# Coefficients of an expert layer's second product, made in pairs of blocks and in place

## The chip, the cores and the metric

The kernel runs on one core of a Trainium2 chip. The metric is the time of one execution on the device, in microseconds; the median of the runs counts. A core has five engines that run side by side: TensorE (matrix products, PE in the profile), VectorE (DVE), ScalarE (ACT), GpSimd (POOL) and SyncE (SP). Each works through its own queue in order. Transfers between memory and the core run on 16 DMA engines; here SyncE's, ScalarE's and GpSimd's queues issue them.

## The reference

The model has two layers. Each has a mixer (a diagonal state-space part and a forgetting attention) and then an expert layer, "PEER", on 512 tokens of width 1024. The change lies in the expert layer:

```python
t1, i1 = lax.top_k(s1, 16); t2, i2 = lax.top_k(s2, 16)      # per token and head, 8 heads
...
best, pos = lax.top_k(cand, 16)                              # 16 of 16384 experts
gate = jax.nn.softmax(best, axis=-1)
...
act = gelu(einsum('tkd,td->tk', u_tab[idx], h))
out = einsum('tk,tkd->td', act * gate, v_tab[idx])
```

Each token takes 8 x 16 of 16,384 experts, each a row of `u_tab` and one of `v_tab`, and sums the rows of `v_tab` with the coefficients `gelu(u . h) * gate`.

## The kernel before, in words

The 512 tokens are four blocks of 128. For three of them (384 tokens, `NT`) the kernel computes the expert layer densely: all 16,384 experts, in 128 blocks of 128 (`NBLK`), with a gate that is zero for an expert that a token did not take. The fourth block of tokens gathers its rows one by one (`gather_step`, lines 974 to 986): an indirect load on GpSimd, a dot product on VectorE (line 995), a gelu and a scale on ScalarE (lines 996, 997) and a sum on VectorE (line 998). These steps are spread over the whole layer.

The dense part has two products. The first (`u_stage`, lines 928 to 938) makes, for one block of experts, the activations of 384 tokens: 128 partitions (experts) by 384 columns (tokens), gelu on ScalarE. For the first 116 blocks (`NAHEAD`, called `M`) this is done ahead, while the routing and the gates are computed, and the activations are written to memory (`ad`). The last 12 blocks, here called late, run inside the second part: their activations stay on the core.

The gates (`gates`) are written to memory as `gd`, laid out by 12 groups of 32 tokens, 128 experts of a block, 128 blocks, 32 tokens.

The second product (phase "two", lines 1051 to 1117) goes through an order of 140 steps, `order`: a late `u`, then 9 or 10 of the early `v` blocks, then the late `v`, twelve times over. For each `v` block:

- `gate_of` and `act_of` load gates and activations for four blocks at a time, on ScalarE's queue, each into one of two buffers (`g0`, `ar`); late gates go, also by four, into the one buffer `g1`. They are called for the block itself and up to four (`PF`) blocks on. `s.after(s.marks[0])` puts such an issue behind the last block's rounding on ScalarE.
- `v_coef` (lines 950 to 963) multiplies activation and gate on VectorE into `c` (one buffer, line 958), rounds it on ScalarE to the high half of `cc` (line 960), and subtracts on VectorE to get the low half (line 961). `cc` has three buffers of one block.
- `v_block` (lines 965 to 972) issues 6 matmuls for each of the three blocks of tokens, 18 in all, adding into six banks of PSUM, with the weights split the same way: `hi` on ScalarE (line 168), `lo` on VectorE or, for every fourth block, on GpSimd (line 169). `raw` has five buffers, loaded by SyncE (line 160); `hi` and `lo` have three each, and the next block's are made while one is in use.

In layer 0 the preparation of layer 1's state-space part (`s5_prep`) runs in small pieces in the same phase, mostly on VectorE, with small stores on ScalarE's queue. The order of the instructions on each engine is made by the framework: it takes the ready instruction of the highest priority in a run of its own clock. `high_priority(offset=AHEAD)` lets splits and coefficients go ahead of their place. A tile with `bufs=n` is handed out again once everything that used it is done.

```python
def v_coef(s, act, gate):
    c = s.t("c", [1, NT])
    cc = s.t("cc", [2, NT], F32R, bufs=3)
    ...
```

Of the kernel before, what the change touches and what calls it, by code (L numbers as in the profile page):

```python
# [9 lines left out]
F32R = mybir.dt.float32r  # L10
# [3 lines left out]
AF = mybir.ActivationFunctionType  # L14
OP = mybir.AluOpType
# [8 lines left out]
NT = 384  # L24
# [22 lines left out]
class Net:  # L47
# [899 lines left out]
                s.gather_step()  # L947
            yield

    def v_coef(s, act, gate):  # L950

        nc = s.nc
        v = nc.vector
        c = s.t("c", [1, NT])
        cc = s.t("cc", [2, NT], F32R, bufs=3)
        ch, cl = cc[:, 0], cc[:, 1]
        with s.tc.high_priority(offset=AHEAD):
            v.tensor_tensor(c[:, 0].rearrange("p (g t) -> p g t", t=32), act.rearrange("p (g t) -> p g t", t=32),  # L958
                            gate, op=OP.mult)
            on_act = nc.scalar.activation(ch, c[:, 0], AF.Copy)  # L960
            on_dve = v.tensor_tensor(cl, c[:, 0], ch, op=OP.subtract)  # L961
        s.marks = on_act, on_dve
        return ch, cl

    def v_block(s, w, c, tb, first, last):
        wh, wl = w
# [33 lines left out]
    def peer(s, prep_next):  # L1000
        nc, a, l = s.nc, s.a, s.l
# [10 lines left out]
        M = NAHEAD  # L1012
# [9 lines left out]
        ad = s.dr.tile([M, 128, NT], F32, name=f"ad{l}", tag="ad")  # L1022
# [28 lines left out]
        with s.phase("two"):  # L1051
            for _ in up:
                pass
            s.pv = [[s.p("pb"), s.p("pb")], [s.p("pb"), s.p("pb")], [s.p("pc"), s.p("pc")]]
            G, A = {}, {}

            def gate_of(b):
                key = (b // 4, b < M)
                if key not in G:
                    g = s.t("g0" if b < M else "g1", [NT // 32, 4, 32], bufs=2 if b < M else 1)  # L1060
                    q = b - b % 4
                    nc.scalar.dma_start(g, s.gd[:, :, q:q + 4].rearrange("g p i t -> p g i t"))
                    G[key] = g
                return G[key][:, :, b % 4]

            def act_of(b):
                if b >= M:
                    return A.pop(b)
                if b // 4 not in A:
                    t = s.t("ar", [4, NT], bufs=2)  # L1070
                    q = b - b % 4
                    nc.scalar.dma_start(t, ad[q:q + 4].rearrange("b p t -> p b t"))
                    A[b // 4] = t
                return A[b // 4][:, b % 4]

            nv = 0
            tail = []
            vs = [b for kd, b in order if kd == "v"]
            prep = iter(())
            if prep_next:  # L1080
                prep = s.s5_prep(l + 1, (nc.vector,), "pa", 1)
            for i, (kd, b) in enumerate(order):
                w = next(ws)
                if kd == "u":
                    o = s.ga.tile([128, NT], F32, name=f"au{l}_{b}", tag="ao", bufs=3)
                    s.u_stage(w, o)
                    A[b] = o
                else:
                    for fb in vs[nv:nv + PF + 1]:
                        with ExitStack() as st:  # L1090
                            if nv:
                                st.enter_context(s.after(s.marks[0]))
                            gate_of(fb)
                            if fb < M:
                                act_of(fb)
                    c = s.v_coef(act_of(b), gate_of(b))
                    nv += 1
                    if nv <= NBLK - TAIL:
                        for tb in range(NTB):
                            s.v_block(w, c, tb, nv == 1, False)  # L1100
                    else:
                        tail.append((w, c))
                gl = 128 + GLAG - GA
                if (i + 1) * gl // GEND > i * gl // GEND:
                    s.gather_step()
                if i >= 24 and i % PREPSTEP == 0:
                    with s.after(s.marks[0]), s.after(s.marks[1]):
                        next(prep, None)
            while s.gk < 128 + GLAG:
                s.gather_step()  # L1110
            list(prep)
            for tb in range(NTB):
                for j, (w, c) in enumerate(tail):
                    s.v_block(w, c, tb, False, j == TAIL - 1)
                for hf in range(2):
                    hs = s.h[:, tb, 512 * hf:512 * hf + 512]
                    nc.vector.tensor_tensor(hs, s.pv[tb][hf], hs, op=OP.add)
# [91 lines left out]
```

## Time and profile before

| | |
|---|---|
| median of 3 runs | 3212.95 us (3211.52 to 3228.48) |
| the profiled execution | 3227.44 us |
| its span, first to last instruction | 3225.7 us |
| mean granted TensorE clock | 0.986 |
| busy: TensorE, VectorE, ScalarE, GpSimd | 3111.4, 2379.7, 1156.8, 841.5 us |
| moved by DMA | 810.92 MB, 251 GB/s |

The span is one execution; the engines overlap, so the busy times do not add up to it. An engine's idle time counts only where another that sets the end waits for it. A matmul is pipelined: its busy time says when the array was occupied, not at what rate, so counts of matmuls in a stretch are the better measure of progress. "Granted clock" is the share of full speed at which TensorE was allowed to run. In rows about queues, ACTq is ScalarE's queue: the time an issue of a transfer holds it.

### The profile page before, as it was taken

What the parts mean: (1) busy time and instruction counts of PE and PEld (TensorE: products, weight loads), DVE (VectorE), ACT (ScalarE), POOL (GpSimd) and SP (SyncE); (2) the same over time, 40 slices, a digit from 0 to 9 for tenths busy, and PEclk for the clock granted to TensorE, in tenths of its full rate; (3) what the DMA queues carried; (4) which work ended last, traced back from release to release, by engine and by line L of the source; (5) the groups of instructions that cost most, each with busy time, mean ns of one, the idle gap of its engine ahead of it and who ended that gap; (6) DMA issues with size and microseconds to landing.
All of it is one profiled execution on the core that took longest, in us unless ns stands there. A gap on an engine that the chain in (4) does not pass through costs nothing. (4 is left out here: it accounts for less than half of the span.)

```text
span 3225.7 us, 43367 instructions
## 1 busy us (share of the span) xinstructions
PE 3111.4 (96%) x15858; PEld 2449.3 (76%) x15858; DVE 2379.7 (74%) x5007; ACT 1156.8 (36%) x2192; POOL 841.5 (26%) x488
## 2 busy tenths in 40 slices
PE   8999998999999998999999999989999999999998
PEld 7756755677999777787889576546779987788887
DVE  7654697977545798998767647979766367788887
ACT  3263212333333343444342531123333333334443
POOL 3100012101675332343210000210027742233231
PEclk9999998999999999999999999999999999999999
DMA  6511278767898889999963123887579889999995
GB/s 185 195 54 58 92 266 306 251 225 267 310 302 307 306 309 308 346 333 334 331 211 104 40 79 97 296 301 248 208 276 321 287 303 320 324 330 344 333 344 208
DMA packets 354726, 810.92 MB, mean 251 GB/s; under 512 B 22833, under 2 KB 228657, under 8 KB 318673
## 3 DMA queue, kind: packets, MB, share of 16 engines
q1 hardware_dynamic: 136608, 326.23, 30.5%
q0 software_dynamic: 36864, 268.45, 22.2%
q10 hardware_dynamic: 181040, 213.48, 19.7%
q8 instruction: 124, 2.03, 0.3%
q14 instruction: 90, 0.73, 0.1%
HBM read 693.19 MB, written 114.82 MB: 250 GB/s over the span
## 5 line engine op out<-in xcount | busy, mean ns | idle before, releaser
L169 POOL TENSOR_TENSOR lo<-raw,hi 128x1024 fp32r<-128x1024 f32 x160 | 429.5, 2688 | 1082.6 <-ACT hi L168 961.0
L168 ACT ACTIVATE hi<-raw 128x1024 fp32r<-128x1024 f32 x425 | 448.1, 1055 | 518.0 <-PE pc L971 167.4
L971 PE MATMUL pb<-hi,cc 128*128 128x512 f32 x2048 | 610.1, 399 | 24.6 <-ACT cc L960 18.7
L983 POOL DMA_INDIRECT ruv<-in_peer_uv_dram,idx x256 | 362.4, 1416 | 717.1 <-DVE h L998 313.3
L995 DVE SCALAR_TENSOR_TENSOR ruv<-ruv,hn 128x1024 f32<-128x1024 f32 x256 | 339.2, 1328 | 246.5 <-DMA ruv<-in_peer_uv_dram,idx 245.8
L971 PEld LDWEIGHTS pb<-hi,cc 128*128 128x128 f32 x2048 | 384.5, 189 | 122.3 <-ACT cc L960 23.9
L998 DVE SCALAR_TENSOR_TENSOR h<-ruv,gc,h 128x1024 f32<-128x1024 f32 x256 | 387.9, 1515 | 84.6 <-ACT gc L997 83.0
L169 DVE TENSOR_TENSOR lo<-raw,hi 128x1024 fp32r<-128x1024 f32 x265 | 327.1, 1235 | 152.4 <-ACT hi L168 152.2
L935 PE MATMUL pa<-xf,raw 128*128 128x384 f32 x1088 | 370.3, 492 | 0.6 <-ACT ao L938 0.6
L935 PE MATMUL pc<-xf,raw 128*128 128x384 f32 x1088 | 368.4, 490 | 0.9 <-ACT ao L938 0.9
L971 PE MATMUL pb<-lo,cc 128*128 128x512 f32 x1024 | 325.3, 398 | 6.7 <-DVE lo L169 6.6
L971 PE MATMUL pc<-hi,cc 128*128 128x512 f32 x1024 | 324.5, 397 | 2.7 <-ACT ao L938 2.7
L935 PEld LDWEIGHTS pc<-xf,raw 128*128 128x128 f32 x1088 | 205.2, 191 | 138.9 <-issue 4.1
L935 PEld LDWEIGHTS pa<-xf,raw 128*128 128x128 f32 x1088 | 205.0, 192 | 136.3 <-issue 2.0
L996 ACT ACTIVATE gc<-gc 128x1 f32<-128x1 f32 x256 | 51.3, 200 | 591.9 <-DVE ruv L995 572.0
L971 PEld LDWEIGHTS pb<-lo,cc 128*128 128x128 f32 x1024 | 193.0, 190 | 56.9 <-DVE lo L169 11.1
L971 PEld LDWEIGHTS pc<-hi,cc 128*128 128x128 f32 x1024 | 193.7, 189 | 50.0 <-ACT ao L938 3.6
L961 DVE TENSOR_TENSOR cc<-c,cc 128x384 fp32r<-128x384 f32 x256 | 187.0, 730 | 42.2 <-ACT cc L960 42.0
L960 ACT ACTIVATE cc<-c 128x384 fp32r<-128x384 f32 x256 | 132.7, 518 | 220.7 <-DVE c L958 200.8
L203 PE MATMUL pa<-x,hi 128*128 128x384 f32 x576 | 198.5, 345 | 2.9 <-ACT hi L168 2.9
L205 PE MATMUL pa<-x,lo 128*128 128x384 f32 x576 | 196.2, 341 | 4.6 <-POOL lo L169 3.8
L204 PE MATMUL pa<-x,hi 128*128 128x384 f32 x576 | 192.7, 335 | 0.0
(340 smaller groups left out, 5164.5 us busy)
## 6 DMA issues: line engine op xcount, KB each, us to landing
raw<-in_peer_uT_dram SPq DMA_DIRECT2D x256, 512.0 KB, 4.6
raw<-in_peer_uv_dram SPq DMA_DIRECT2D x256, 512.0 KB, 6.9
gd<-t ACTq DMA_DIRECT2D x24, 2048.0 KB, 6.5
g<-gd ACTq DMA_DIRECT2D x64, 768.0 KB, 9.8
ad<-ao ACTq DMA_DIRECT2D x232, 192.0 KB, 6.2
ar<-ad ACTq DMA_DIRECT2D x58, 768.0 KB, 9.6
raw<-in_w_in_dram SPq DMA_DIRECT2D x34, 512.0 KB, 6.9
s5p<-pE ACTq DMA_DIRECT2D x16, 512.0 KB, 3.9
```

Source lines behind the costliest of these rows:

```text
L168: s.nc.scalar.activation(hi, raw, AF.Copy)
L169: ins = eng.tensor_tensor(lo, raw, hi, op=OP.subtract)
L203: mm(ps, lh, rh, start=start, stop=False)
L204: mm(ps, lh, rl, start=False, stop=False)
L205: return mm(ps, ll, rh, start=False, stop=stop)
L935: s.umark = nc.tensor.matmul(po, wh[:, k], s.xf[:, :, k], start=(k == 0), stop=(k == 7))
L960: on_act = nc.scalar.activation(ch, c[:, 0], AF.Copy)
L961: on_dve = v.tensor_tensor(cl, c[:, 0], ch, op=OP.subtract)
L971: s.nc.tensor.matmul(s.pv[tb][hf], x[:, sl], y[:, 512 * hf:512 * hf + 512], start=(first and e == 0), stop=(last and e == 2))
L983: nc.gpsimd.indirect_dma_start(out=r, out_offset=None, in_=a["uv_flat"], in_offset=off)
L995: v.scalar_tensor_tensor(ru, ru, 1.0, s.hn, op0=OP.mult, op1=OP.mult, accum_out=c[:, 0:1])
L998: v.scalar_tensor_tensor(acc, rv, c[:, 2:3], acc, op0=OP.mult, op1=OP.add)
```

## The change

A pair of neighbouring early blocks now gets its coefficients in one go: one product, one rounding, one subtraction over 2 x 384 columns. The product is written over the activations themselves, in `ar`. `cc` has two buffers of a pair. The late blocks keep single coefficients with `c` and a buffer `cd` of their own. The gates of the late blocks are loaded one block at a time into two buffers; those of the early blocks still by four. `marks` is set once for a pair.

```diff
-    def v_coef(s, act, gate):
+    def v_coef(s, tag, bufs, c, act, gate):
...
-        c = s.t("c", [1, NT])
-        cc = s.t("cc", [2, NT], F32R, bufs=3)
-        ch, cl = cc[:, 0], cc[:, 1]
+        n = c.shape[1]
+        cc = s.t(tag, [2, n, NT], F32R, bufs=bufs)
+        g = lambda x: x.rearrange("p b (g t) -> p b g t", t=32)
         with s.tc.high_priority(offset=AHEAD):
-            v.tensor_tensor(c[:, 0].rearrange("p (g t) -> p g t", t=32), act.rearrange("p (g t) -> p g t", t=32),
-                            gate, op=OP.mult)
-            on_act = nc.scalar.activation(ch, c[:, 0], AF.Copy)
-            on_dve = v.tensor_tensor(cl, c[:, 0], ch, op=OP.subtract)
+            v.tensor_tensor(g(c), g(act), gate.rearrange("p g b t -> p b g t"), op=OP.mult)
+            on_act = nc.scalar.activation(cc[:, 0], c, AF.Copy)
+            on_dve = v.tensor_tensor(cc[:, 1], c, cc[:, 0], op=OP.subtract)
         s.marks = on_act, on_dve
-        return ch, cl
+        return [(cc[:, 0, j], cc[:, 1, j]) for j in range(n)]
...
             def gate_of(b):
-                key = (b // 4, b < M)
-                if key not in G:
-                    g = s.t("g0" if b < M else "g1", [NT // 32, 4, 32], bufs=2 if b < M else 1)
-                    q = b - b % 4
-                    nc.scalar.dma_start(g, s.gd[:, :, q:q + 4].rearrange("g p i t -> p g i t"))
-                    G[key] = g
-                return G[key][:, :, b % 4]
+                n = 4 if b < M else 1
+                q = b - b % n
+                if q not in G:
+                    g = s.t("g0" if b < M else "g1", [NT // 32, n, 32], bufs=2)
+                    nc.scalar.dma_start(g, s.gd[:, :, q:q + n].rearrange("g p i t -> p g i t"))
+                    G[q] = g
+                return G[q]
 
             def act_of(b):
+                q = b - b % 4
+                if q not in A:
+                    t = s.t("ar", [4, NT], bufs=2)
+                    nc.scalar.dma_start(t, ad[q:q + 4].rearrange("b p t -> p b t"))
+                    A[q] = t
+                return A[q]
+
+            def coef_of(b):
                 if b >= M:
-                    return A.pop(b)
...
+                    c = s.t("c", [1, NT])
+                    return s.v_coef("cd", 1, c, A.pop(b)[:, None, :], gate_of(b))[0]
+                if b not in C:
+                    j = b % 4
+                    x = act_of(b)[:, j:j + 2]
+                    C[b], C[b + 1] = s.v_coef("cc", 2, x, x, gate_of(b)[:, :, j:j + 2])
+                return C.pop(b)
...
-                    c = s.v_coef(act_of(b), gate_of(b))
+                    c = coef_of(b)
```

## Rows read from the trace of the kernel before

**Rows 1.** The page: busy time, share of the span and instructions of each engine.
```profile
PE 3111.4 (96%) x15858; PEld 2449.3 (76%) x15858; DVE 2379.7 (74%) x5007; ACT 1156.8 (36%) x2192; POOL 841.5 (26%) x488
```

**Rows 2.** Windows, layer 1: length, busy time (instructions) by engine, clock, DMA share, GB/s.
```profile
2840.00:2890.00 50.00, 50.00 (x222) 41.06 (x221) 41.46 (x48) 20.06 (x36) 18.00 (x10) 1.00 0.98 345
```

**Rows 3.** Windows of layer 0's second product, the same columns (PE, PEld, DVE, ACT, POOL).
```profile
1110.00:1160.00 50.00, 50.00 (x222) 41.11 (x221) 46.64 (x94) 25.88 (x45) 15.98 (x9) 1.00 0.81 282
1160.00:1210.00 50.00, 47.07 (x205) 37.48 (x204) 47.18 (x149) 19.13 (x34) 15.11 (x10) 1.00 0.89 319
1210.00:1260.00 50.00, 41.83 (x176) 33.21 (x175) 47.10 (x81) 18.11 (x33) 15.87 (x7) 0.97 0.95 334
```

**Rows 4.** Waits of TensorE, whole run: us in total, times, longest us.
```profile
PE pb L971 <- ACT cc L960: 18.7, 10, 3.8
...
PE pb L971 <- DVE lo L169: 6.6, 5, 2.3
...
PE pb L971 <- ACT hi L168: 4.4, 6, 1.7
```

**Rows 5.** TensorE in order of time: start, length, what, in brackets idle before.
```profile
1104.96 1.22 PE L971 MATMUL pb<-hi,cc 128*128 128x512 f32 x2 [3.83 <-ACT cc L960]
...
1259.77 0.73 PE L971 MATMUL pb<-hi,cc 128*128 128x512 f32 x2 [3.13 <-ACT cc L960]
...
2703.42 1.22 PE L971 MATMUL pb<-hi,cc 128*128 128x512 f32 x2 [3.45 <-ACT cc L960]
```

**Rows 6.** ScalarE and its queue in order of time, ahead of two of these.
```profile
1095.94 7.40 ACTq L1072 DMA_DIRECT2D ar<-ad  x1
1103.44 1.06 ACT L168 ACTIVATE hi<-raw 128x1024 fp32r<-128x1024 f32 x1 [7.38 <-issue]
...
2701.90 1.06 ACT L168 ACTIVATE hi<-raw 128x1024 fp32r<-128x1024 f32 x1 [7.62 <-issue]
```

**Rows 7.** Single lines: count, duration ns min/median/max, first and last start, forms.
```profile
L958 DVE TENSOR_TENSOR c<-ar,g x232: 537/557/2795, 839.7 to 3201.5; 128x384 f32<-128x384 f32 x116
...
L961 DVE TENSOR_TENSOR cc<-c,cc x256: 543/552/2770, 843.0 to 3206.5; 128x384 fp32r<-128x384 f32 x128
...
L960 ACT ACTIVATE cc<-c x256: 504/525/531, 842.4 to 3205.5; 128x384 fp32r<-128x384 f32 x128
...
L169 DVE TENSOR_TENSOR lo<-raw,hi x265: 1203/1221/2641, 161.4 to 3205.4; 128x1024 fp32r<-128x1024 f32 x133
...
L168 ACT ACTIVATE hi<-raw x425: 1039/1060/1071, 159.7 to 3203.7; 128x1024 fp32r<-128x1024 f32 x142
```

**Rows 8.** The page's group (busy, mean ns, idle before); then GpSimd and VectorE by time.
```profile
L961 DVE TENSOR_TENSOR cc<-c,cc 128x384 fp32r<-128x384 f32 x256 | 187.0, 730 | 42.2 <-ACT cc L960 42.0
...
1199.93 3.56 POOL L169 TENSOR_TENSOR lo<-raw,hi 128x1024 fp32r<-128x1024 f32 x1 [9.85 <-DVE pX L394]
...
1201.17 2.74 DVE L961 TENSOR_TENSOR cc<-c,cc 128x384 fp32r<-128x384 f32 x1
```

**Rows 9.** ScalarE and VectorE in order of time: a rounding and its subtraction.
```profile
1175.71 0.53 ACT L960 ACTIVATE cc<-c 128x384 fp32r<-128x384 f32 x1
...
1180.40 0.55 DVE L961 TENSOR_TENSOR cc<-c,cc 128x384 fp32r<-128x384 f32 x1
```

**Rows 10.** Issues of gates and activations on ScalarE's queue, columns as in rows 7.
```profile
L1062 ACTq DMA_DIRECT2D g<-gd x64: 366/366/2431, 817.1 to 3162.2; - x64
...
L1072 ACTq DMA_DIRECT2D ar<-ad x58: 501/1703/8392, 817.5 to 3162.7; - x58
```

**Rows 11.** DMA queues, 2640 to 3216 us: ScalarE's queue, packets, MB, share of 16 engines.
```profile
q10 hardware_dynamic: 57766, 43.21, 25.2%
```

More of the change, by code (lines that the diff above doesn't have):

```diff
@@ L1054, in peer @@
             s.pv = [[s.p("pb"), s.p("pb")], [s.p("pb"), s.p("pb")], [s.p("pc"), s.p("pc")]]
-            G, A = {}, {}
+            G, A, C = {}, {}, {}
             def gate_of(b):
-                key = (b // 4, b < M)
-                if key not in G:
-                    g = s.t("g0" if b < M else "g1", [NT // 32, 4, 32], bufs=2 if b < M else 1)
-                    q = b - b % 4
-                    nc.scalar.dma_start(g, s.gd[:, :, q:q + 4].rearrange("g p i t -> p g i t"))
-                    G[key] = g
-                return G[key][:, :, b % 4]
-            def act_of(b):
-                if b >= M:
-                    return A.pop(b)
[L1069 to L1074, printed above, removed]
+                n = 4 if b < M else 1
[5 more added lines that the diff above has]
+                return G[q]
+            def act_of(b):
+                q = b - b % 4
[5 more added lines that the diff above has]
+            def coef_of(b):
+                if b >= M:
+                    c = s.t("c", [1, NT])
[5 more added lines that the diff above has]
+                return C.pop(b)
             nv = 0
```

## The prediction, made before the changed kernel was built or run

> **What bounds the kernel now.** I read the page first. TensorE is busy for 96% of the span, VectorE for 74%, ScalarE for 36% [rows 1], so a part that only spares VectorE or ScalarE is worth something only where TensorE stands still for them. The change touches nothing but the coefficients of the second product, so the next view is the table of windows over the two stretches in which that product runs: about 1020 to 1650 us in layer 0 and 2622 to 3216 us in layer 1. A stretch in which nothing is late shows 222 matmuls in 50 us at a granted clock of 1.00, the 2.4 GHz level [rows 2]. That is 0.225 us a matmul and 18 x 0.225 = 4.05 us for one block of the second product. Layer 1 holds this from 2790 us to the end. Layer 0 does not: between 1110 and 1260 us, where the preparation of the next layer runs on VectorE, VectorE is busy for 46.64 + 47.18 + 47.10 = 140.9 of 150 us and TensorE starts 222 + 205 + 176 = 603 matmuls instead of 666, a loss of 63 x 0.225 = 14.2 us [rows 3].
>
> The table of waits then says what was late. Over the whole run TensorE waited in the second product 18.7 us for the rounded coefficient `cc` from ScalarE, 6.6 us for the low half of the weights and 4.4 us for the high half [rows 4]. That is all there is to win: 29.7 us. A wait costs more than its length: in 1210 to 1260 us TensorE idles 50 - 41.83 = 8.17 us but is 46 matmuls short, 10.4 us [rows 3], a factor of 1.27.
>
> The chart in order of time shows why `cc` is late. Three of its ten waits, 3.83 + 3.13 + 3.45 = 10.4 us, are the largest [rows 5], and in two of them I followed ScalarE back: its queue stood 7.40 us in the issue of one load of activations, `ar`, and the first thing after it was not `cc` but a high half of the weights, which ended at 1103.44 + 1.06 = 1104.50 us, and in the other at 2701.90 + 1.06 = 2702.96 us [rows 6]. TensorE went on 0.46 us after each. There the coefficient was the last thing late, and the weights were late with it.
>
> **The change, part by part.**
>
> *Two blocks in one instruction.* Before, a pair of blocks costs VectorE two products at 0.557 and two subtractions at 0.552 us, and ScalarE two roundings at 0.525 us. After, it is one each, over 768 columns. A line through the subtraction of 384 columns (0.552) and that of 1024 (1.221) gives 0.552 + 384 x 0.669/640 = 0.953 us; for ScalarE, through 0.525 and 1.060, 0.846 us [rows 7]. Bounds: no less than one old instruction, no more than two. I take the lines. A pair saves VectorE 2.218 - 1.906 = 0.31 us and ScalarE 0.20 us; 58 pairs a layer make 36 us and 23 us in both layers. The 12 late blocks of a layer stay single. What of it lies on the path: TensorE itself does the same matmuls, so only the stretch where VectorE is nearly full pays. It holds 603/18 = 33 blocks, nearly 17 pairs: 17 x 0.31 = 5.2 us. The rest hides behind TensorE; without that cover it would be a gain, not a cost.
>
> VectorE's subtraction also shows a median of 0.552 us, a mean of 0.730 and a longest of 2.77 us [rows 7, 8]. One of the long ones started at 1201.17 us, in the middle of GpSimd's own subtraction of the weights (1199.93 to 1203.49 us), and ended just behind it [rows 8]. The excess is 256 x 0.178 = 45.6 us in both layers. The Trainium skill (GPSIMD Engine Reference, Specifications) says that GpSimd shares its SBUF interfaces with VectorE and contends with VectorE instructions that have two SBUF inputs. The row agrees. If such collisions went with the number of starts, 256 to 140, another 20.7 us of VectorE time would go, 150/1224 of it in the full stretch, and the sum below would be 2.5 us better. I leave it out, since a longer instruction is also longer in the way.
>
> *Two buffers of pairs for three of single blocks.* Before, the rounding of block b+3 may start when TensorE has finished block b: two blocks, 8.1 us, are left. After, the rounding of the pair after next may start when a pair is finished, with one pair, again 8.1 us, left. So the shortest lead is the same, but it is met once in two blocks, and late blocks no longer take a place in the ring. The product is made in place and no longer waits for the one buffer `c`. What this gains at the three large waits is only what lies between the weights and the coefficient: 3 x 0.46 = 1.4 us (the third taken like the other two). Next late are the weights. The remaining 8.3 us of waits for `cc` lie nearly all in the full stretch and are in the 5.2 us.
>
> *Activations held longer.* `ar` is now freed by the subtraction of its second pair, before by the last product. The next load of `ar` on ScalarE's queue waits for that. Of this wait the trace of before shows nothing, as the product always came ahead of the rounding on that queue. Bounds: nothing, if ScalarE reaches the load later than VectorE the subtraction (it stands idle 64% of the time [rows 1]); at worst the distance from a rounding to its subtraction, and one row shows 1180.40 - 1176.22 = 4.2 us [rows 9]. A gain is excluded, as the load is never freed earlier. Queued behind it stand the weights' roundings, and TensorE behind these. I take nothing, since the writer of the queues places the load where its buffer is due, and keep 4.2 us for a rival.
>
> *Late gates one by one.* Per layer, 12 loads of 128-byte runs take the place of 3 loads of 512-byte runs, each with 128 x 12 = 1536 runs. That is 18 more issues on ScalarE's queue, 0.366 us each [rows 10]. An `ar` issue takes 0.50 us at best, 1.70 in the median and 8.39 at worst, because it stands right behind a load of gates [rows 10]. A late load stands alone, but may stand in the way of the next. The 58 `ar` issues brought TensorE the 10.4 us of the three large waits, or 0.18 us each. At that price 18 loads cost 3.2 us. Bounds: nothing, or 18 of the largest, 18 x 3.83 = 69 us.
>
> The transfers themselves: in layer 1's stretch ScalarE's queue moved 57,766 packets at 25.2% of 16 engines' 576 us, which is 40.2 ns for one of 748 B on average [rows 11]. A run of 128 B costs at most that, at least its share of the bytes, 6.9 ns. A 512 B run costs 27.5 ns by its share. I take that for the 128 B run too: 9 x 1536 x 27.5/16 = 24 us more of all engines' time per layer, bounds 0 and 38 us, hidden while the engines are idle for some 5% of 594 us, 30 us (0.81 to 0.98 busy in the windows [rows 2, 3]). The Trainium skill speaks against this part: DMA: Bandwidth & Descriptors, Specifications, gives 512 B as the least transfer at line rate. No row here times a 128 B read alone. By that page the short run is no cheaper than the long one, so the sum would be the same and the cover thinner.
>
> **Sum:** -5.2 - 1.4 + 3.2 = -3.4 us. The profiled execution took 3227.4 us and lies 14.5 us above the median, 3212.95 us, of the runs; taken from the median that is 3209.5 us.
>
> **The rivals.**
> *Everything waits less (faster).* If the shorter work of VectorE lets ScalarE run ahead, the weights come earlier as well, for they stand in the same queue. Then all waits for `cc` go, 18.7 x 1.27 = 24 us: 3189 us. For it: in 1110 to 1260 us every engine but TensorE queues behind VectorE. Against it: the three large waits come from issue, which the change does not touch.
> *The `ar` load holds ScalarE (slower).* If on the chip the subtraction is later than the queue's order supposes, the load waits up to 4.2 us ahead of an issue of 1.7 us. From a stop of about 8.1 us, two blocks' lead, on, TensorE feels it. With the price of the issue scaled, 10.4 x 4.2/1.7 = 26 us: 3236 us. For it: rows 9. Against it: ScalarE's free time.
> *Transfers become the bound (slower).* At 38 us more per layer the idle share is overdrawn by 8 us and the rest arrives later; a third of it seen by TensorE makes 2 x 38/3 = 25 us: 3235 us. Against it: only 18 loads, spread over 1200 us.
> *The pairs save nothing*, 768 columns taking 1.10 us: then the sum is 5.2 us worse, +1.8 us, still inside the forecast's case.
>
> **How the numbers follow.** A measurement of this kernel tells about 0.5% from no change: 16 us, so 3197 to 3229 us is the same. Forecast, small change either way: 0.46. Everything waits less: 0.32, since the loss in layer 0 is real and VectorE is what is eased. `ar` holds ScalarE: 0.14. Transfers: 0.08. The range, 3182 to 3240 us, goes from a little past the faster rival to a little past the slower ones.
>
> **What would show it.** Products and subtractions near 0.95 us, x116 of 768 columns, and 24 late ones; 82 loads of gates; VectorE's busy time lower by some 36 us; the waits of TensorE for `cc` in 1110 to 1260 us smaller, those behind long `ar` issues still there, now named after the weights. I am wrong if the large waits vanish, or if ScalarE shows stops at the `ar` load that end with a subtraction, or if the DMA share stands at 0.99 and waits for weights multiply.

## The result, and the profile after

The changed kernel takes 3239.83 us in the median (3222.37 to 3255.28), the kernel before on the same chip 3220.26 us: a ratio of 1.0064, interval 1.0038 to 1.0091. It is slower by 0.64%, a little more than the 0.5% that a measurement of this kernel can tell from no change. The profiled execution, 3255.3 us, is the slowest of its five.

The single instructions of the change cost what was forecast. First the page's engine line, then single lines (count, duration in ns min/median/max, first and last start):

```profile
PE 3117.3 (96%) x15858; PEld 2453.4 (75%) x15858; DVE 2338.3 (72%) x4775; ACT 1135.6 (35%) x2076; POOL 844.2 (26%) x488
```

```profile
L958 DVE TENSOR_TENSOR ar<-ar,g x116: 942/951/3175, 841.4 to 3207.1; 128x768 f32<-128x768 f32 x116
...
L959 ACT ACTIVATE cc<-ar x116: 822/830/852, 844.6 to 3223.2; 128x768 fp32r<-128x768 f32 x116
...
L960 DVE TENSOR_TENSOR cc<-ar,cc x116: 944/952/3171, 845.5 to 3224.4; 128x768 fp32r<-128x768 f32 x116
...
L1061 ACTq DMA_DIRECT2D g<-gd x82: 366/366/2701, 816.5 to 3206.4; - x82
...
L1069 ACTq DMA_DIRECT2D ar<-ad x58: 366/922/9157, 817.0 to 3186.0; - x58
L1069 ACTq EVENT_SEMAPHORE  x26: 17/17/17, 846.0 to 3124.3; - x26
```

A pair costs 0.951, 0.830 and 0.952 us, and VectorE is busy 41.4 us less [rows 1]. The last two lines already hold the bad news. 26 extra waits for a semaphore now stand ahead of issues of `ar`, 5 before:

```profile
L1072 ACTq EVENT_SEMAPHORE  x5: 17/17/17, 1134.5 to 3124.9; - x5
```

And the median of an issue is 0.92 us instead of 1.70 [rows 10]: before, 57 of the 58 came less than 5 us behind an issue of gates, now 42 do, and the other 16 hold the queue for 0.41 us in the median.

The windows show where it was won and lost (columns as in the windows of before):

```profile
1110.00:1160.00 50.00, 46.63 (x196) 36.87 (x195) 37.72 (x68) 22.88 (x35) 11.36 (x6) 0.97 0.85 304
1160.00:1210.00 50.00, 50.00 (x222) 41.16 (x221) 49.97 (x147) 19.90 (x33) 20.04 (x10) 1.00 0.95 331
1210.00:1260.00 50.00, 47.54 (x207) 38.13 (x207) 49.93 (x79) 18.81 (x30) 15.72 (x9) 1.00 0.91 326
...
2740.00:2790.00 50.00, 43.82 (x179) 34.00 (x177) 28.22 (x28) 14.33 (x23) 15.48 (x9) 0.97 0.90 321
2790.00:2840.00 50.00, 43.17 (x179) 36.03 (x180) 39.09 (x40) 16.88 (x28) 14.13 (x8) 0.90 0.83 278
```

Layer 0's full stretch starts 196 + 222 + 207 = 625 matmuls instead of 603 [rows 3], 22 x 0.225 = 5.0 us. That is a gain of 48 in the second and third window and a loss of 26 in the first. But layer 1 has two windows of 179, where the kernel before had 198 and 220:

```profile
2740.00:2790.00 50.00, 46.03 (x198) 37.23 (x197) 35.77 (x43) 17.04 (x30) 16.26 (x9) 0.98 0.86 305
2790.00:2840.00 50.00, 50.00 (x220) 41.17 (x220) 43.82 (x55) 22.38 (x40) 15.16 (x9) 0.99 0.94 336
```

From the first to the last matmul of L970 (L971 before), layer 1 took 614.9 us instead of 600.9, layer 0 632.0 instead of 628.4.

The tables of waits name the new stop: first TensorE's, then VectorE's, after the change and before it, then ScalarE's from 2622 us on (us in total, times, longest us).

```profile
PE pa L205 <- DVE lo L169: 13.3, 5, 8.8
...
PE pb L970 <- POOL lo L169: 6.9, 6, 1.8
...
PE pb L970 <- DVE cc L960: 3.1, 4, 1.3
...
PE pb L970 <- ACT cc L959: 2.0, 2, 1.5
```

```profile
DVE ar L958 <- DMA ar<-ad: 46.4, 10, 14.0
```

```profile
DVE c L958 <- DMA ar<-ad: 11.2, 4, 5.8
```

```profile
ACT hi L168 <- issue: 63.5, 14, 12.1
ACT hi L168 <- DVE cc L960: 35.4, 6, 17.0
```

TensorE's waits for the rounded `cc` fell from 18.7 us to 2.0 [rows 4]. In their place VectorE waits 46.4 us for activations that have not landed (11.2 us before), and ScalarE stands up to 17.0 us until a subtraction. Of ScalarE's two lines only the second is new: the one that ends with "issue" had 63.9 us before. The largest case, in order of time, on ScalarE and its queue, then on VectorE, then on TensorE:

```profile
2771.31 0.37 ACTq L1061 DMA_DIRECT2D g<-gd  x1
2771.40 1.05 ACT L168 ACTIVATE hi<-raw 128x1024 fp32r<-128x1024 f32 x1
2771.70 1.57 ACTq L1069 DMA_DIRECT2D ar<-ad  x1
...
2797.67 0.37 ACTq L1069 DMA_DIRECT2D ar<-ad  x1
2798.14 1.06 ACT L168 ACTIVATE hi<-raw 128x1024 fp32r<-128x1024 f32 x1 [17.01 <-DVE cc L960]
```

```profile
2793.81 1.83 DVE L958 TENSOR_TENSOR ar<-ar,g 128x768 f32<-128x768 f32 x2 [13.99 <-DMA ar<-ad]
2795.55 1.22 DVE L169 TENSOR_TENSOR lo<-raw,hi 128x1024 fp32r<-128x1024 f32 x1
2796.69 0.95 DVE L960 TENSOR_TENSOR cc<-ar,cc 128x768 fp32r<-128x768 f32 x1
```

```profile
2796.83 0.69 PE L205 MATMUL pa<-x,lo 128*128 128x384 f32 x1 [8.82 <-DVE lo L169]
```

A load issued at 2771.70 us landed 22 us later. VectorE stood at its product for 13.99 us. Behind it stood the low half that TensorE needed (L205 is here a matmul of a late `u`), and TensorE lost 8.82 us. Behind it stood also the subtraction that frees the other buffer of `ar`; the next load waited for that on ScalarE's queue until 2797.67 us, and behind the load the high halves of the weights. The stop has an echo in the clock: its mean is 0.97 in the window of the stop and 0.90 in the next, so part of these stretches ran below the 2.4 GHz level (1.00) of a stretch without stops [rows 2].

### The profile page after: what moved, and what is told of

The parts are those of the page before. It is cut to its first block, busy times and chain, and to the rows that moved or that the text cites. A ratio compares the mean times of both kernels' runs of the same rounds, so it can differ in the third digit from the quotient of the medians.

```text
span 3253.5 us, 42954 instructions
## 1 busy us (share of the span) xinstructions
PE 3117.3 (96%) x15858; PEld 2453.4 (75%) x15858; DVE 2338.3 (72%) x4775; ACT 1135.6 (35%) x2076; POOL 844.2 (26%) x488
## 3 DMA queue, kind: packets, MB, share of 16 engines
q10 hardware_dynamic: 208976, 213.48, 19.8%
## 5 line engine op out<-in xcount | busy, mean ns | idle before, releaser
L982 POOL DMA_INDIRECT ruv<-in_peer_uv_dram,idx x256 | 369.0, 1441 | 820.2 <-DVE h L997 427.1
L970 PE MATMUL pb<-hi,cc 128*128 128x512 f32 x1856 | 553.3, 399 | 9.2 <-ACT hi L168 3.8
L970 PEld LDWEIGHTS pb<-hi,cc 128*128 128x128 f32 x1856 | 350.4, 190 | 94.9 <-DVE cc L960 6.4
L970 PE MATMUL pb<-lo,cc 128*128 128x512 f32 x928 | 295.9, 400 | 12.0 <-POOL lo L169 6.9
L970 PE MATMUL pc<-hi,cc 128*128 128x512 f32 x928 | 293.1, 396 | 1.3 <-ACT ao L938 1.3
L970 PEld LDWEIGHTS pb<-lo,cc 128*128 128x128 f32 x928 | 174.7, 190 | 58.7 <-POOL lo L169 9.5
L205 PE MATMUL pa<-x,lo 128*128 128x384 f32 x576 | 199.2, 346 | 17.1 <-DVE lo L169 13.3
L970 PEld LDWEIGHTS pc<-hi,cc 128*128 128x128 f32 x928 | 175.0, 189 | 43.9 <-ACT ao L938 1.7
L892 DVE TENSOR_TENSOR o<-oh,idt 128x1024 bf16<-128x1024 bf16 x288 | 180.3, 685 | 0.0
L890 DVE TENSOR_TENSOR oh<-iota,idt 128x1024 bf16<-128x1024 bf16 x192 | 127.6, 711 | 64.3 <-PE pb L902 64.3
```

The costliest lines, as they stand in the source:

```text
L205: return mm(ps, ll, rh, start=False, stop=stop)
L890: v.tensor_tensor(oh[:, i], s.iota2[:, None].to_broadcast([128, 4, 128, 2]), col(i), op=OP.is_equal)
L892: v.tensor_tensor(o3[:, i], oh[:, 0], col(2 + i), op=OP.mult)
L970: s.nc.tensor.matmul(s.pv[tb][hf], x[:, sl], y[:, 512 * hf:512 * hf + 512], start=(first and e == 0), stop=(last and e == 2))
L982: nc.gpsimd.indirect_dma_start(out=r, out_offset=None, in_=a["uv_flat"], in_offset=off)
```

## The experiments

All ratios are against the kernel before, run beside it on the same chip. "Hold" is the time that the issues of `ar` hold ScalarE's queue, added up over the rows of both second products, by my own adding: 141 us before, 95 after. It is the queue's time: ScalarE may meanwhile finish what it was handed earlier. "Stop" is the time that ScalarE and its queue stand idle right ahead of an issue of `ar`, added up in the same way: 0 before, 85 us after, in 27 issues, up to 16.5 us.

**The parts alone.** First the pairs with their product in a tile of its own, otherwise as changed:

```diff
+                    c = s.t("c2", [2, NT])
-                    C[b], C[b + 1] = s.v_coef("cc", 2, x, x, gate_of(b)[:, :, j:j + 2])
+                    C[b], C[b + 1] = s.v_coef("cc", 2, c, x, gate_of(b)[:, :, j:j + 2])
```

> The pairs as in the changed kernel, but the product goes into a tile of its own, one buffer of two blocks, so that the activations are free again after the product and not after the subtraction. Theory 'held too long' (the activations are freed late, so their next load holds ScalarE's queue and lands late, and VectorE's product waits for it at the head of its queue): back within 0.2% of before (ratio 0.995 to 1.002), VectorE's wait for the activations' load below 15 us in all (46.4 us in the changed kernel) and ScalarE's waits behind the subtraction nearly gone. Theory 'late gates' (18 more loads): still 1.005 or more. Theory 'pairs in a burst' (two blocks at once make each miss longer): still 1.005 or more, with VectorE's waits for the load small.

Measured: 1.0069 (1.0044 to 1.0095). VectorE's wait for `ar` is down to 5.2 us, and nothing is won: the hold is 185 us, and TensorE waits 11.2 us for `cc` from ScalarE again. So writing in place is not the cause by itself. The stops are gone (0 us), so holding the activations longer in two buffers does make them; without them the issues hold the queue twice as long.

Late gates block by block, nothing else of the change:

```diff
-                key = (b // 4, b < M)
+                n = 4 if b < M else 1
+                q = b - b % n
...
-                    g = s.t("g0" if b < M else "g1", [NT // 32, 4, 32], bufs=2 if b < M else 1)
+                    g = s.t("g0" if b < M else "g1", [NT // 32, n, 32], bufs=2)
```

> The kernel before with one part of the change alone: the gates of the late blocks loaded block by block into two buffers. Theory 'late gates': ratio 1.004 or more, with more or longer holds of ScalarE's queue at the load of activations than the 58 with a median of 1.70 us before. The other theories: 0.998 to 1.002; the prediction's own price was 3 us, 1.001.

Measured: 1.0065 (1.0047 to 1.0082), 21 us, with layer 1 even shorter (592.5 us) and layer 0 longer (647.3 us). My term for it was 3.2 us.

The changed kernel with late gates by four, as before:

```diff
-                n = 4 if b < M else 1
-                q = b - b % n
+                q = b - b % 4
...
-                    g = s.t("g0" if b < M else "g1", [NT // 32, n, 32], bufs=2)
+                    g = s.t("g0" if b < M else "g1", [NT // 32, 4, 32], bufs=2 if b < M else 1)
```

> The changed kernel with the late gates loaded by four again, as before. Theory 'late gates': back to 1.000 to 1.002. 'Held too long' and 'pairs in a burst': stays at 1.004 to 1.009, VectorE's wait for the load of activations stays above 30 us.

Measured: 1.0089 (1.0070 to 1.0108). Taking out a part that costs 0.65% alone gave nothing back: the parts do not add up.

The kernel before with the product in place, single blocks:

```diff
-        c = s.t("c", [1, NT])
+        c = s.t("c", [1, NT]) if own else act[:, None, :]
```

> The kernel before, block by block, with three single buffers for the rounded halves, but the product of an early block written over its activations. Theory 'held too long': 1.003 to 1.008, as the activations of four blocks are now freed by the last subtraction, and VectorE waits for their load more than the 11.2 us of before. 'Late gates' and 'pairs in a burst': 0.998 to 1.002.

Measured: 1.0037 (1.0023 to 1.0051). VectorE's wait rises to 81.7 us, the largest of all, and TensorE waits for the low half what it no longer waits for the coefficient (before 6.6 and 18.7 us, [rows 4]):

```profile
DVE ar L958 <- DMA ar<-ad: 81.7, 15, 11.7
```

```profile
PE pb L971 <- DVE lo L169: 29.9, 10, 6.9
```

The pairs alone, in a tile of their own, late gates by four (the edits of the first and the third of these runs together):

> Pairs and two buffers of pairs alone: the product in a tile of its own (one buffer, which the late blocks share), the late gates by four as before. Theory 'pairs in a burst': 1.004 or more, with TensorE's waits for cc and the halves longer but not more numerous. If the loss of the kernel with pairs in a tile of their own (1.0069) came from its late gates: 0.997 to 1.002.

Measured: 1.0085 (1.0065 to 1.0106), VectorE's wait 55.0 us though nothing is in place, the hold 180 us.

Each part also reshuffles the queues. Two controls change only when things come: one shifts the gather steps a little (`GEND` 137), one asks for gates and activations five blocks ahead.

```diff
-GEND = 136
+GEND = 137
```

```diff
-PF = 4
+PF = 5
```

> A control: the kernel before with the gather's steps spread over 137 in place of 136 steps of the order, so that some of them come one step later and the queues' order changes, but nothing is computed, loaded or held differently. Theory 'the order before is a good one by luck': 1.003 or more. Theory 'each part of the change has a cost of its own': 0.998 to 1.002.

> A second control: the kernel before with gates and activations asked for five blocks ahead in place of four (two buffers each as before, so a load can still not start before its buffer is free). Theory 'the order before is a good one by luck': 1.003 or more. Otherwise 0.997 to 1.002.

Measured: 1.0010 (0.9995 to 1.0025) and 1.0041 (1.0021 to 1.0060). A new order alone is worth 0.1% to 0.4%; single differences of that size prove nothing here, and the 0.37% of the product in place alone is such a one.

**More buffers, asked for earlier.** If loads land late because their buffer is held, a third buffer should help. A first try also put the late products in place:

```diff
-                    t = s.t("ar", [4, NT], bufs=2)
+                    t = s.t("ar", [4, NT], bufs=3)
...
-                    c = s.t("c", [1, NT])
-                    return s.v_coef("cd", 1, c, A.pop(b)[:, None, :], gate_of(b))[0]
+                    c = A.pop(b)[:, None, :]
+                    return s.v_coef("cd", 1, c, c, gate_of(b))[0]
```

> The changed kernel with three buffers for the activations of four blocks in place of two; to make room the late blocks' products are written over their activations too, so that the buffer c is gone. Theory 'held too long': with a third buffer the load no longer depends on the subtraction just made, so VectorE's wait for the load falls below 10 us (46.4 in the changed kernel), ScalarE's stops behind the subtraction go, and the ratio is 0.3% or more better than the changed kernel's 1.0064: 0.998 to 1.003. Theory 'any other order of the queues is worse than the one before by 0.4 to 0.9%': the wait goes and the ratio stays at 1.004 to 1.009, the loss standing in waits for the weights' halves and for cc instead.

Measured: 1.0210 (1.0188 to 1.0232), slower than either theory said. As two things had changed, the third buffer was tried by itself (`g1` with one buffer, for room):

> The changed kernel with three buffers of activations in place of two (to have the room, the late gates get one buffer in place of two). The loads are still asked for four blocks ahead. Theory A (a load comes too late for its product because it is asked for late: four blocks, some 16 us): a third buffer alone changes little; VectorE's wait for the activations stays over 30 us in all and the ratio to the kernel before stays at 1.004 to 1.010. Theory B (a load comes late because its buffer is held until the subtraction of the pair before): with a third buffer no load has to wait for a subtraction; VectorE's wait falls below 10 us and the ratio to 1.003 or less.

Measured: 1.0191 (1.0167 to 1.0214), VectorE's wait 61.1 us, the hold 197 us, no stop. The wait is theory A's, the ratio lies above what both gave. And with `PF = 6`:

> As the run with three buffers of activations, and gates and activations asked for six blocks ahead instead of four. Theory A (asked for too late): VectorE's wait for the activations falls below 10 us, TensorE's waits for the low half of the weights below 8 us in all, and the ratio to the kernel before is 1.002 or less. If VectorE's wait goes and the ratio stays at 1.005 or more, that wait was not what the change cost, and the rest lies in the order of the queues or in the late gates.

Measured: 1.0225 (1.0204 to 1.0246). My lead theory of that moment, late loads alone, falls here: VectorE's wait does drop to 19.3 us, and the kernel is the slowest of all. TensorE now waits for the high half of the weights (27.4 us in 11), and ScalarE's queue shows why:

```profile
1153.08 7.20 ACTq L1069 DMA_DIRECT2D ar<-ad  x1
...
1154.81 0.83 ACT L959 ACTIVATE cc<-ar 128x768 fp32r<-128x768 f32 x1
1160.33 4.24 ACTq L1061 DMA_DIRECT2D g<-gd  x1
1164.66 5.29 ACTq L1069 DMA_DIRECT2D ar<-ad  x1
1170.05 1.06 ACT L168 ACTIVATE hi<-raw 128x1024 fp32r<-128x1024 f32 x1 [14.41 <-issue]
```

```profile
1171.16 1.22 PE L970 MATMUL pb<-hi,cc 128*128 128x512 f32 x2 [7.06 <-ACT hi L168]
```

With a third buffer the stops are nearly gone (4 us), and each issue instead holds the queue while it is made: a median of 5.0 us, 250 us in all. A load on this queue costs either way: asked for early it holds ScalarE, asked for late it lands late.

**The late loads.** In the kernel before with late gates one by one, each load was first made long: the whole group of four, in runs of 512 bytes.

```diff
-                    nc.scalar.dma_start(g, s.gd[:, :, q:q + n].rearrange("g p i t -> p g i t"))
+                    q4 = b - b % 4
+                    nc.scalar.dma_start(g, s.gd[:, :, q4:q4 + 4].rearrange("g p i t -> p g i t"))
```

> The kernel before with late gates loaded for each block on its own, as in the run of that part alone (ratio 1.0065), but each of these loads carries the whole group of four blocks, in runs of 512 bytes, into one buffer: as many loads on ScalarE's queue, four times the bytes, no short runs. Theory short runs (runs of 128 bytes disturb the other transfers): the ratio falls back to 1.002 or less. Theory number of loads (18 more issues on ScalarE's queue, and the order of the queues that they bring): it stays at 1.004 to 1.008.

Measured: 1.0131 (1.0110 to 1.0152), above both theories. The short runs are thus not shown to be the cost; what makes this run dearer is open, as it has four times the bytes and also one buffer where the short loads have two. TensorE waits 22.4 us for the high half of the weights in it. Then the short loads on SyncE's queue:

```diff
-                    nc.scalar.dma_start(g, s.gd[:, :, q:q + n].rearrange("g p i t -> p g i t"))
+                    (nc.scalar if b < M else nc.sync).dma_start(g, s.gd[:, :, q:q + n].rearrange("g p i t -> p g i t"))
```

> The kernel before with late gates loaded for each block on its own in runs of 128 bytes into two buffers, but issued by SyncE's queue instead of ScalarE's. Theory holds (each more issue on ScalarE's queue may stop ScalarE's own work): the ratio falls to 1.002 or less, and TensorE's wait for the coefficient in layer 0 from 20 us to 12 us or less. Theory short runs or order of the queues: it stays at 1.004 or more. If SyncE's own loads of weights are held up behind them, the waits for the halves of the weights grow, and the ratio goes above 1.008.

Measured: 1.0018 (1.0005 to 1.0031), TensorE's wait for the coefficient in layer 0 14.9 us instead of 20.0, not the 12 expected. With the queue 0.47 of the 0.65% went, which is little more than the larger control; by itself it does not prove the queue.

**The queue.** So the loads were moved to SyncE, which does nothing but issue. In the changed kernel the late gates alone:

> The changed kernel with only the loads of late gates, still one block each, moved from ScalarE's queue to SyncE's. Theory parts: the late loads cost because they stand on ScalarE's queue (alone 0.65%, and 0.18% when SyncE issues them); taking them off leaves the in-place part: ratio to the kernel before 1.002 to 1.005, VectorE's wait for the activations still over 30 us. Theory no sum: beside the in-place product the late loads cost nothing of their own, and the ratio stays at 1.006 or more.

Measured: 1.0085 (1.0065 to 1.0105), VectorE's wait 70.6 us. No gain: the early loads still have both prices. Then all of them, in the changed kernel, in the one with three buffers and six blocks ahead, and in the kernel before:

```diff
-                    nc.scalar.dma_start(g, s.gd[:, :, q:q + n].rearrange("g p i t -> p g i t"))
+                    nc.sync.dma_start(g, s.gd[:, :, q:q + n].rearrange("g p i t -> p g i t"))
...
-                    nc.scalar.dma_start(t, ad[q:q + 4].rearrange("b p t -> p b t"))
+                    nc.sync.dma_start(t, ad[q:q + 4].rearrange("b p t -> p b t"))
```

> The changed kernel with all loads of gates and activations moved from ScalarE's queue to SyncE's; buffers and the four blocks ahead as they are. Theory ScalarE's queue (the load of activations either holds ScalarE while it is issued or stands on its queue until a subtraction and then lands late): ScalarE's waits that end with the subtraction are gone, VectorE's wait for the activations falls from 46 us to 25 us or less, and the ratio to the kernel before is 1.002 or less. Theory early product (in place, the product comes to the head of VectorE's queue too early, whatever queue loads): VectorE's wait stays over 40 us and the ratio at 1.005 or more. If SyncE's loads of weights are held up behind the new ones, TensorE waits for the halves of the weights more than before, and the ratio goes above 1.01.

> The run with three buffers of activations asked for six blocks ahead (ratio 1.0225 with ScalarE's queue, issues of activations holding it 250 us in all, VectorE's wait 19 us), all loads of gates and activations moved to SyncE's queue. Theory ScalarE's queue: both costs are gone, VectorE's wait is below 20 us, TensorE's wait for the high half of the weights falls from 27 us to 8 us or less, and the ratio to the kernel before is 1.000 or less. If it stays above 1.01, the holds on ScalarE's queue were not what that run cost; contention of the transfers or the order of the queues is left.

> The kernel before with all loads of gates and activations moved from ScalarE's queue to SyncE's. It tells what the queue is worth by itself, so that the two runs above are read rightly. Theory ScalarE's queue: TensorE's wait for the coefficient falls from 18.7 us to below 10 us, the ratio is 0.994 to 0.999. Theory hidden: those holds lie beside other work, and the ratio stays within 0.002 of 1; or SyncE's weights are held up, and it is above 1.005.

Measured: 0.9959 (0.9944 to 0.9974), 0.9962 (0.9948 to 0.9976) and 0.9967 (0.9951 to 0.9983). The changed kernel gets 1% faster by this one move, the run with three buffers 2.6%. VectorE's wait in the changed kernel is 9.7 us instead of 46.4. And beside the kernel before with the same move the whole change now costs nothing. TensorE's wait for the coefficient in that kernel is 11.3 us, not below 10 as expected. Stops ahead of `ar` are still there in the changed kernel, 64 us, but on SyncE's queue they stop no computing engine. The loads do not land sooner: in the kernel before the median from issue to landing is 9.6 us on ScalarE's queue and 9.8 on SyncE's.

Last, the same move for two parts alone, to see that no two prices cancel there:

> The run of the pairs alone (product into a tile of its own, late gates by four; ratio 1.0085 with ScalarE's queue), all loads of gates and activations on SyncE's queue. Theory ScalarE's queue: the price of the pairs was that of their loads on that queue; the ratio to the kernel before is 0.994 to 0.999, like the kernel before with the same move (0.9967), and VectorE's wait for the activations falls from 55 us to 15 us or less. Rival: pairs have a price of their own (a longer product behind which the low halves queue): ratio 1.002 or more.

> The run of the product in place alone (single blocks; ratio 1.0037 with ScalarE's queue, VectorE's wait for the activations 82 us), all loads of gates and activations on SyncE's queue. Theory ScalarE's queue: VectorE's wait falls to 20 us or less and the ratio is 0.994 to 0.999. Rival early product: the product in place still comes to the head of VectorE's queue ahead of its activations, VectorE's wait stays over 40 us, ratio 1.001 or more.

Measured: 0.9908 (0.9892 to 0.9924) and 0.9939 (0.9920 to 0.9958), VectorE's wait 0 and 21.3 us. The pairs alone, with SyncE's queue, are the best kernel of the study: 3189.8 us against 3219.4. Their windows of layer 0 and the largest of TensorE's waits in the second product (L970):

```profile
1110.00:1160.00 50.00, 50.00 (x222) 41.06 (x221) 41.56 (x77) 25.80 (x40) 12.73 (x8) 1.00 0.93 333
1160.00:1210.00 50.00, 50.00 (x222) 41.06 (x221) 49.97 (x136) 18.04 (x30) 19.20 (x11) 1.00 0.96 348
1210.00:1260.00 50.00, 49.62 (x218) 40.20 (x217) 49.86 (x86) 19.52 (x31) 15.85 (x7) 1.00 1.00 344
```

```profile
PE pb L970 <- DVE lo L169: 2.2, 2, 1.5
...
PE pb L970 <- ACT hi L168: 0.3, 1, 0.3
```

222 + 222 + 218 = 662 matmuls of 666. The kernel before with the same move has 214 + 201 + 187 = 602 there, so the queue does not fill this stretch; the pairs do. They are not the only way: the product in place of single blocks brings it to 215 + 213 + 213 = 641. The two windows that show it, of the kernel before and of the product in place, both on SyncE's queue:

```profile
1210.00:1260.00 50.00, 45.02 (x187) 36.29 (x186) 46.96 (x91) 17.16 (x32) 13.11 (x7) 0.93 0.83 294
```

```profile
1210.00:1260.00 50.00, 48.37 (x213) 39.35 (x212) 50.00 (x75) 20.06 (x38) 14.51 (x7) 1.00 0.91 315
```

## Why the prediction was wrong

The kernels that bear on the cause side by side; stop, hold and VectorE's wait in us:

| kernel | stop ahead of `ar` | hold of ScalarE's queue | VectorE waits for `ar` | ratio |
|---|---|---|---|---|
| before | 0 | 141 | 11 | 1 |
| after | 85 | 95 | 46 | 1.0064 |
| after, late gates by four | 67 | 103 | 51 | 1.0089 |
| after, late gates on SyncE's queue | 76 | 135 | 71 | 1.0085 |
| pairs in own tile, late gates single | 0 | 185 | 5 | 1.0069 |
| pairs alone | 0 | 180 | 55 | 1.0085 |
| late gates single, alone | 5 | 118 | 5 | 1.0065 |
| in place alone | 19 | 50 | 82 | 1.0037 |
| three buffers | 0 | 197 | 61 | 1.0191 |
| three buffers, six blocks ahead | 4 | 250 | 19 | 1.0225 |

With all these loads on SyncE's queue neither stop nor hold falls on ScalarE:

| kernel, loads on SyncE's queue | VectorE waits for `ar` | ratio |
|---|---|---|
| before | 0 | 0.9967 |
| after | 10 | 0.9959 |
| three buffers, six blocks ahead | 3 | 0.9962 |
| in place alone | 21 | 0.9939 |
| pairs alone | 0 | 0.9908 |

**The step that failed** is "Activations held longer ... I take nothing". The runs show 85 us of stops in its place, where the kernel before has none, and they come with the product in place in two buffers: the kernels without it have at most 5 us. The bound of 4.2 us was the distance from a rounding to its subtraction in a row where VectorE was working [rows 9]. It does not hold when VectorE itself stands at a product whose activations are late: then the subtraction, the next load behind it and the weights' roundings behind that all wait, 17.0 us in the case shown. And the reason, that the writer of the queues places the load where its buffer is due, was an argument about a plan, not a row. VectorE's own wait for the load, 46.4 us, had no term at all, though 11.2 us of it stood in the table before.

That term is not all that failed. With the product in a tile of its own the activations are freed as before, the stops are gone, and the pairs still cost 0.7% to 0.85%: the hold rises from 141 us to 180 and 185. So the premise that the issues are what "the change does not touch" failed too, and with it the reading of the pairs as "a gain, not a cost".

The rival that came nearest is "the `ar` load holds ScalarE" (chance 0.14), and its sign in the trace, stops of ScalarE that end with a subtraction, is there. It named the place. That its price of 26 us comes near the 19.6 us measured is luck: it is scaled from a single distance of 4.2 us and leaves out VectorE's wait.

**Two blocks in one instruction**: the cost of the instructions was right. 0.953 and 0.846 us were forecast, 0.951 and 0.830 measured; 36 us less of VectorE, 41.4 measured. The collisions with GpSimd, rightly left out, did not go with the number of starts: the excess of the subtractions over their median is still 36.6 us, after 45.6. That the 5.2 us for the full stretch met 5.0 is luck, for the 5.0 are a gain of 48 matmuls, 10.8 us, less a loss of 26, 5.9 us, in fixed windows, and the whole second product of layer 0 became 3.6 us longer. What was too low is what pairs can bring once nothing else stands in the way. On SyncE's queue they take 3207.4 us (0.9967) to 3189.8 us (0.9908), 0.6% or 19 us by the ratios. This is what the rival "everything waits less" (24 us) describes: in the trace TensorE no longer waits for `cc` at all. I set it aside because of the waits that come from issue; those had to go first.

**Two buffers of pairs**: the waits for `cc` went almost wholly, more than the 1.4 us I allowed, but what is late next is the low half of the weights, not the high half that I named.

**Late gates one by one**: the sign was right, the size was not. 3.2 us came from an average price of an issue; alone the part costs 21 us, on SyncE's queue 6 us (0.18%), and in company none that can be told. An average price per issue says little when the same issue takes 0.5 to 8.4 us [rows 10].

**The transfers**: not the bound. ScalarE's queue moved 208,976 packets in 19.8% of 16 engines' span, 181,040 in 19.7% before. That is 0.198 x 3253.5 - 0.197 x 3225.7 = 8.7 us more of all engines' time for both layers (5 to 12 with the rounding of the shares), where I had 48. For 27,936 more packets and the same bytes that is 16 x 8.7 us / 27,936 = 5.0 ns a packet, where I took 27.5. The Trainium skill (DMA: Bandwidth & Descriptors, Specifications) gives 512 bytes as the least transfer at line rate. From this the prediction concluded that a short run is no cheaper than a long one; by the trace it is, though dearer than its share of the bytes: with 27.5 ns for a long run, four short ones come to an estimated 27.5 + 3 x 5.0 = 42.5 ns, 10.6 each. And with SyncE's queue the pairs start 662 of 666 matmuls at a DMA share of 0.93 to 1.00.

**The cause that the runs show** is the queue. Loads of gates and activations stand on the queue of an engine whose next work TensorE waits for. The Trainium skill (Trainium Kernel Development and Optimization, Key Constraints) says that spreading issues over engines saves only the issue time. The trace agrees in that the loads land no sooner, 9.6 and 9.8 us in the median; but that time was here 50 to 250 us of ScalarE's queue. Moving the loads, which takes the stops away with it, was worth 0.3% before the change, 1% after it and 2.6% with three buffers asked for six blocks ahead. Shown is that the whole change, the pairs, the product in place and these three buffers, which all cost time with ScalarE's queue, cost none with SyncE's. That a new order alone explains this is unlikely: five kernels of five different orders went the same way, four of them by 1.0% to 2.6%, where the controls moved 0.1% and 0.4%, and neither control made the kernel faster. The 0.3% of the kernel before is no more than a control's. Which of stop, hold and late landing each kernel paid for is read from the traces, not tried one by one.

**What stays open**: why late gates alone cost 0.65% with a shorter hold (118 us) and VectorE waiting only 5 us; the longest stop of TensorE there, 5.6 us, followed a store of the next layer's preparation that held ScalarE 7.6 us behind a load of gates, but that is one place. Stop, hold and wait together go the right way, 152 us before, 226 after, 235 for the pairs alone, 258 and 273 with three buffers, but they are no price: the product in place alone has 151 and late gates alone 128, and both are slower than before. And why the whole change on SyncE's queue (0.9959) is slower than its pairs alone (0.9908) was not taken apart; the traces show that TensorE waits 9.6 us there for the subtraction of `cc`, and not at all with the pairs alone.

## What to carry to other kernels

A load on the queue of an engine that computes is paid for either way: asked for early it holds the engine while it is issued, asked for late, or behind a buffer that is still in use, it makes the engine and the reader stand. On a queue that only issues, hold and stop cost no computing engine anything here, and the reader's wait was 0 to 21 us. When a buffer is freed later than before, follow the load that waits for it and everything behind it on that queue, and ask also what stands behind the reader. And before a part of a change is called cheap or dear, run it alone and in company, with a control that only changes the order.

## What was not expected of the hardware

The time that one and the same load holds its queue goes from 0.46 to 11.4 us (`ar` on ScalarE's queue with three buffers), and is mostly long when a load of gates was issued less than 5 us before: in the kernel with six blocks ahead once 0.39 us for the gates and 6.18 us for the activations behind them, and 0.38 to 0.46 us for the three loads without gates so close. On SyncE's queue it is no shorter in the pairs' kernel, a median of 3.35 us and up to 7.57 (2.18 and 11.85 on ScalarE's), but there it hides:

```profile
L1068 SPq DMA_DIRECT2D ar<-ad x58: 427/3349/7567, 820.7 to 3119.6; - x58
```

A load of 768 KB that was issued in 1.57 us took until 22 us after its issue to be used, at a DMA share of 0.94 in that time; in the kernel before `ar` landed 7.9 to 14.7 us after its issue. A distance of four blocks, 4 x 4.05 = 16.2 us, does not cover that.
